# Handing out the 16 memory-projection tiles in the loop over the delta-rule chunks

## The chip, the cores and the metric

The kernel runs on one core of a Trainium2 chip. The metric is device time in microseconds of one execution. Each core has five engines with in-order instruction queues of their own: TensorE (PE, matrix products; PEld is its weight load), VectorE (DVE), ScalarE (ACT), GpSimd (POOL) and SyncE (SP), which here issues every DMA. Matrix products accumulate in PSUM banks; everything else lies in SBUF or in DRAM.

## The reference

One decoder layer over 1024 tokens of width 1024, float32. A mixer with two halves side by side (a gated delta rule over four heads, and an S5 state-space model over 512 channels with a gate), then cross-attention to 256 memory tokens, then a SwiGLU block:

```python
h = x
h = h + _mixer(_rmsnorm(h, norm_mix_g), ...)          # [delta-rule heads | S5 channels] @ w_out
h = h + _cross_attn(_rmsnorm(h, norm_x_g), mem, ...)
h = h + _swiglu(_rmsnorm(h, norm_ffn_g), ...)
return _rmsnorm(h, norm_final_g)

def _cross_attn(hn, mem, norm_mem_g, w_xq, w_xk, w_xv, w_xo):
    mn = _rmsnorm(mem, norm_mem_g)                    # 256 x 1024
    q = hn @ w_xq
    k = mn @ w_xk                                     # the memory projections:
    v = mn @ w_xv                                     # 256 x 1024 each
    s = q k^T / 16;  p = softmax(s);  return (p v) @ w_xo
```

The memory projections `k` and `v` depend on the memory tokens and on their two weights alone, not on `x`.

## The kernel before

**Numbers.** A float32 operand is split into a rounded high part and the remainder (`split`: ScalarE writes the high part, VectorE or GpSimd subtracts), and a product is three matmuls, high x high, high x low, low x high (`mm3`). `weight` loads one 128-column slice of a weight (512 KB) into `wraw` (two buffers) and splits it into `whi` and `wlo` (three buffers each); its last argument names the engine that subtracts. All these lie in the pool `wp`, which lives for the whole kernel, as do three PSUM banks `mm` in the pool `pm`.

**Order.** Instructions are written in program order, and the framework's planner (the tile context is opened with its timeline simulation) then orders each engine's queue at build time: an instruction that is earlier in the program has the higher rank, but one of lower rank goes ahead where the planner's simulated times and the free buffers allow it. On the chip each queue is worked off in that fixed order. A buffer is handed on when its readers are done, and a pool's room when the pool is closed.

**Stages around the change**, in program order in `emit`:

1. The delta-rule heads: projections (`in_tile`), `dn_a`, `dn_v`, `dn_b` for four heads; `mem_prep` before them normalises the memory tokens and leaves their split parts `mh`, `ml` in eight temporary tiles of 128 x 512 (`fsg`, `sq`, `res`, `acc0`, `acc1`), two of the eight 128-row slices in each.
2. The loop over the eight chunks of 128 tokens (line 1473). `dn_seq(c)` loads the chunk's matrices (`d_X4`, `d_kT`, `d_N3`) and goes through four dependent products with the state (lines 747, 755, 761 and 771/772), with VectorE (749, 764) and ScalarE (756) between them; `dn_tail(c - 1)` normalises and gates the chunk before and writes its split parts into `AH` and `AL`.
3. The eight S5 blocks: `s5_in` (loads `s_W`, `s_U`, `s_M`, `s_T`, matmuls, evacuation) and `s5_out` (mostly VectorE and GpSimd, lines 389 to 406; matmuls 411 and 412), with `glu_in` after every second one. The planner mixes stages 2 and 3.
4. `seq.close()` ends the chunks' pools `dp` and `sq` (`dq` in the code); the pool `kv` then opens on the same side. `glu` computes the S5 gate.
5. `mem_proj` twice, for `w_xk` and `w_xv`: eight tiles each. A tile loads and splits a weight slice (GpSimd subtracts), does 24 matmuls of 128 x 256 into an `mm` bank, is copied by ScalarE into `kst` (four buffers, in `kv`), and is stored into `memD` in DRAM.
6. `mem_load` brings the keys back from `memD` and splits them; `out_acts` forms sums and differences of the mixer's output (lines 935 to 949, in `fsg`, `res` and `sq`); `fold_k` multiplies the keys with `w_xq`; `out_pair` follows.

Of the kernel before, what the change touches and what calls it, by code (L numbers as in the profile page):

```python
# [9 lines left out]
F32 = mybir.dt.float32  # L10
F32R = mybir.dt.float32r
I32 = mybir.dt.int32
AF = mybir.ActivationFunctionType
# [5 lines left out]
P = 128  # L19
NT = 1024  # L20
HT = 512
KD = 8
NMEM = 256
# [22 lines left out]
class Kernel:  # L46
# [778 lines left out]
            ml += [two(l)[:, j] for j in range(2)]  # L825
        return mh, ml

    def mem_proj(self, kv, mem, w, dst):

        mh, ml = mem  # L830
        for m in range(KD):
            wh, wl = self.weight(self.I[w][m], KD, P, self.g)
            ps = self.pm.tile([P, HT], F32, name="mm")
            for k in range(KD):
                self.mm3(ps[:, 0:NMEM], wh[:, k], wl[:, k], mh[k], ml[k], k == 0, k == KD - 1)
            t = kv.tile([P, HT], F32, name="kst", bufs=4)[:, 0:NMEM]
            self.a.activation(out=t, in_=ps[:, 0:NMEM], func=AF.Copy)
            self.load(dst[:, m], t)

    def mem_load(self, kv, src):  # L840
        o = [kv.tile([P, KD, NMEM], F32R, name=n) for n in ("kvh", "kvl")]
# [554 lines left out]
    def emit(self, ctx):  # L1396
        tc, nc, I = self.tc, self.nc, self.I
        pool = lambda name, side="left", **k: tc.tile_pool(name=name, side=side, **k)
# [30 lines left out]
        with pool("cv", bufs=1) as cv:  # L1429
# [19 lines left out]
            mem = self.mem_prep(cv)  # L1449
            dp = seq.enter_context(pool("dp", "right", bufs=1))  # L1450
            with psum("pda", 1) as self.pda, psum("pdb", 2) as self.pb:
                with pool("dx", "right", bufs=1) as dx:
                    for hd in range(4):
                        k, q = self.in_tile(4 + hd, cv), self.in_tile(hd, cv)
# [8 lines left out]
        dq = seq.enter_context(pool("sq", "right", bufs=1))  # L1463
# [6 lines left out]
        self.turn = {}  # L1470
        with psum("ps6", 1) as self.p6, psum("pds", 1) as self.ps, psum("pdo", 2) as self.po:
            po = {}
            for c in range(9):
                if c < 8:
                    po[c] = self.dn_seq(c, dq)
                if c > 0:
                    self.dn_tail(c - 1, po[c - 1], dq, xs)
            with pool("s5b", bufs=1) as sb:
                s = self.s5_in(0, sb)
                for b in range(8):  # L1480
                    s2 = self.s5_in(b + 1, sb) if b < 7 else None
                    self.s5_out(b, sb, *s)
                    if b % 2:
                        self.glu_in(b // 2, xs)
                    s = s2
            seq.close()
            kvs = ExitStack()
            kv = kvs.enter_context(pool("kv", "right", bufs=1))
            with pool("q8", bufs=1) as q8:
                self.glu(q8, xs)  # L1490
            self.mem_proj(kv, mem, "w_xk", self.memD[0])
            self.mem_proj(kv, mem, "w_xv", self.memD[1])
        s5p.close()

        self.pa = ctx.enter_context(psum("pa", 5))
# [84 lines left out]
        for i, o in enumerate((slice(0, HT), slice(HT, HT + 256), slice(HT + 256, NT))):  # L1580
            w = o.stop - o.start
# [84 lines left out]
```

## Time and profile before

| | |
|---|---|
| median of 3 runs | 1664.36 us (1663.36 to 1666.16) |
| profiled execution | 1661.97 us, span of its instructions 1660.2 us |
| mean granted TensorE clock | 0.945 |
| busy: TensorE, VectorE, ScalarE, GpSimd | 89%, 74%, 39%, 42% of the span |
| DMA | 237.50 MB, mean 143 GB/s |

The span runs from the first to the last instruction. A busy time counts an engine's instructions that do work; waits are told as the idle time in front of an instruction, with what ended it. Stretches of the span are named in us from its start. In a table of stretches each engine has its busy us and, in brackets, its instructions; then come the granted clock of TensorE (1 is full), the mean busy share of the 16 DMA engines, and what they moved. L835 is line 835 of the kernel.

### The profile page before, as it was taken

Reading aid. Unit: us, or ns where it says so; the run is one execution under the profiler, and the core shown is the slowest. Engines: PE = TensorE matmul, PEld = TensorE weight load, DVE = VectorE, ACT = ScalarE, POOL = GpSimd, SP = SyncE. Lnnn points to the kernel's source line nnn. Section 1 sums busy time; section 2 is a strip of 40 time slices with the busy share of each in tenths; the row PEclk is TensorE's granted clock in tenths of the full one; section 3 lists DMA queues with packets and bytes.
Section 4 is the critical chain, followed back from the end, with each engine's and each line's share of the span. In section 5 each row is a group of like instructions: output and inputs, shape, how many; then the busy total and the mean of one; then the engine's idle time right before and its main releaser. Section 6 shows DMA issues by size and latency. Waiting matters only on the chain. (4 is left out here: it accounts for less than half of the span.)

```text
span 1660.2 us, 20913 instructions
## 1 busy us (share of the span) xinstructions
PE 1480.0 (89%) x7302; PEld 1230.2 (74%) x7302; DVE 1228.8 (74%) x2156; ACT 642.6 (39%) x1144; POOL 696.2 (42%) x507
## 2 busy tenths in 40 slices
PE   6887977987878958999999969999999998999985
PEld 4776766876777857878888758888888886787764
DVE  8958887976898178776555898666666658799985
ACT  5222443342445444355443433233333334533322
POOL 6084433224334554730010464333333337676554
PEclk8998989988889989999999979999999999999997
DMA  6356534345973346335524223444433446544402
GB/s 216 88 159 196 164 103 103 102 116 153 329 248 121 122 145 215 112 105 173 170 89 165 83 89 108 130 137 140 139 128 127 133 148 217 206 140 149 140 10 102
DMA packets 146617, 237.50 MB, mean 143 GB/s; under 512 B 12464, under 2 KB 79440, under 8 KB 143952
## 3 DMA queue, kind: packets, MB, share of 16 engines
q1 hardware_dynamic: 146512, 236.17, 44.4%
q8 instruction: 57, 0.93, 0.2%
q14 instruction: 48, 0.39, 0.1%
HBM read 169.69 MB, written 68.53 MB: 143 GB/s over the span
## 5 line engine op out<-in xcount | busy, mean ns | idle before, releaser
L62 ACT ACTIVATE whi<-wraw 128x1024 fp32r<-128x1024 f32 (+2 forms) x156 | 142.1, 914 | 215.7 <-PE aux L81 59.2
L79 PE MATMUL mm<-AH,whi 128*128 128x512 f32 x436 | 175.7, 403 | 2.2 <-DVE hT L1313 2.2
L81 PE MATMUL mm<-AH,wlo 128*128 128x512 f32 x420 | 168.6, 402 | 0.0
L80 PE MATMUL mm<-AL,whi 128*128 128x512 f32 x396 | 158.9, 402 | 0.0
L147 POOL TENSOR_TENSOR acc<-acc,sq 128x512 f32<-128x512 f32 (+1 forms) x41 | 53.6, 1309 | 216.6 <-ACT sq L146 215.5
L1174 POOL TENSOR_TENSOR sg<-sg,ca 128x512 f32<-128x512 f32 x44 | 64.1, 1459 | 141.2 <-DVE sg L1167 94.8
L63 DVE TENSOR_TENSOR wlo<-wraw,whi 128x1024 fp32r<-128x1024 f32 (+1 forms) x76 | 99.8, 1317 | 31.1 <-ACT whi L62 31.1
L63 POOL TENSOR_TENSOR wlo<-wraw,whi 128x1024 fp32r<-128x1024 f32 x28 | 68.3, 2440 | 130.2 <-ACT whi L62 122.2
L79 PEld LDWEIGHTS mm<-AH,whi 128*128 128x128 f32 x436 | 83.7, 192 | 22.0 <-DVE hT L1313 3.9
L80 PE MATMUL aux<-AL,whi 128*128 128x512 f32 x228 | 90.7, 398 | 5.7 <-POOL AL L63 3.4
L81 PEld LDWEIGHTS mm<-AH,wlo 128*128 128x128 f32 x420 | 80.6, 192 | 18.2 <-issue 0.4
L80 PEld LDWEIGHTS mm<-AL,whi 128*128 128x128 f32 x396 | 76.4, 193 | 16.5
L487 DVE SCALAR_TENSOR_TENSOR it<-pre,convw,it 128x512 f32<-128x512 f32 x72 | 74.8, 1039 | 6.6 <-ACT it L485 5.7
L79 PE MATMUL aux<-AH,whi 128*128 128x512 f32 x188 | 74.6, 398 | 0.3 <-ACT AH L62 0.3
L81 PE MATMUL aux<-AH,wlo 128*128 128x512 f32 x172 | 69.4, 404 | 0.0
L62 ACT ACTIVATE wlo<-graw 128x512 fp32r<-128x512 f32 x66 | 41.3, 626 | 69.8 <-PE aux L81 54.0
L81 PE MATMUL aux<-AH,whi 128*128 128x512 f32 x148 | 58.6, 396 | 0.0
L63 POOL TENSOR_TENSOR wlo<-wb,whi 128x768 fp32r<-128x768 f32 x19 | 39.6, 2084 | 44.2 <-ACT whi L62 44.2
L1172 ACT ACTIVATE ca<-ca 128x512 f32<-128x512 f32 x44 | 27.8, 632 | 77.4 <-DVE ca L1167 76.8
L79 PE MATMUL aux<-AH,wlo 128*128 128x512 f32 x132 | 53.9, 408 | 3.2 <-DVE sq L1167 3.2
L80 PEld LDWEIGHTS aux<-AL,whi 128*128 128x128 f32 x228 | 43.1, 189 | 16.8 <-POOL AL L63 4.3
L80 PE MATMUL aux<-AL,wlo 128*128 128x512 f32 x132 | 53.7, 407 | 0.0
(702 smaller groups left out, 4721.2 us busy)
## 6 DMA issues: line engine op xcount, KB each, us to landing
graw<-in_w_up SPq DMA_DIRECT2D x22, 512.0 KB
actD<-sg SPq DMA_DIRECT2D x44, 256.0 KB
acc<-in_w_down SPq DMA_DIRECT2D x42, 256.0 KB
WD<-acc SPq DMA_DIRECT2D x40, 256.0 KB
wraw<-in_w_in SPq DMA_DIRECT2D x16, 512.0 KB
d_X<-XD SPq DMA_DIRECT2D x8, 1024.0 KB
wraw<-AD SPq DMA_DIRECT2D x16, 512.0 KB
wraw<-VD SPq DMA_DIRECT2D x16, 512.0 KB
```

Of the source, the lines that this page charges most:

```text
L62: self.a.activation(out=hi, in_=src, func=AF.Copy)
L63: return (eng or self.v).tensor_tensor(out=lo, in0=src, in1=hi.bitcast(F32), op=ALU.subtract)
L79: mm(ps, wh, xh, start=first, stop=False)
L80: mm(ps, wh, xl, start=False, stop=False)
L81: mm(ps, wl, xh, start=False, stop=last)
L147: eng.tensor_tensor(out=acc, in0=acc, in1=tmp, op=ALU.add)
L487: v.scalar_tensor_tensor(out=acc, in0=pre[:, 1 + i:1 + i + HT], scalar=cw(i), in1=acc, op0=ALU.mult, op1=ALU.add)
L1172: A.activation(out=r, in_=r, func=AF.Silu)
L1174: g.tensor_tensor(out=r, in0=r, in1=sg[o], op=ALU.mult)
```

## The change

`mem_proj` becomes a generator that does one tile at each step, first the eight of `w_xk`, then the eight of `w_xv`. It is started ahead of the chunk loop and advanced by two tiles in each pass of that loop, after `dn_seq` and `dn_tail`; eight passes use up the 16 tiles. The two calls behind `glu` go. The result tile is now `mst`, 128 x 256, one buffer, in the chunks' pool `sq`, in place of `kst` with four buffers in `kv`.

```diff
-    def mem_proj(self, kv, mem, w, dst):
+    def mem_proj(self, mem, pool):
 
         mh, ml = mem
-        for m in range(KD):
-            wh, wl = self.weight(self.I[w][m], KD, P, self.g)
-            ps = self.pm.tile([P, HT], F32, name="mm")
-            for k in range(KD):
-                self.mm3(ps[:, 0:NMEM], wh[:, k], wl[:, k], mh[k], ml[k], k == 0, k == KD - 1)
-            t = kv.tile([P, HT], F32, name="kst", bufs=4)[:, 0:NMEM]
-            self.a.activation(out=t, in_=ps[:, 0:NMEM], func=AF.Copy)
-            self.load(dst[:, m], t)
+        for w, dst in (("w_xk", self.memD[0]), ("w_xv", self.memD[1])):
+            for m in range(KD):
+                wh, wl = self.weight(self.I[w][m], KD, P, self.g)
+                ps = self.pm.tile([P, HT], F32, name="mm")
+                for k in range(KD):
+                    self.mm3(ps[:, 0:NMEM], wh[:, k], wl[:, k], mh[k], ml[k], k == 0, k == KD - 1)
+                t = pool.tile([P, NMEM], F32, name="mst")
+                self.a.activation(out=t, in_=ps[:, 0:NMEM], func=AF.Copy)
+                self.load(dst[:, m], t)
+                yield
...
             po = {}
+            side = self.mem_proj(mem, dq)
             for c in range(9):
                 if c < 8:
                     po[c] = self.dn_seq(c, dq)
                 if c > 0:
                     self.dn_tail(c - 1, po[c - 1], dq, xs)
+                for _ in range(2):
+                    next(side, None)
...
             with pool("q8", bufs=1) as q8:
                 self.glu(q8, xs)
-            self.mem_proj(kv, mem, "w_xk", self.memD[0])
-            self.mem_proj(kv, mem, "w_xv", self.memD[1])
```

## The prediction

> **What bounds the kernel now.** I read the page's first part, then a table of stretches around the place of the change, then who waited for whom in the stretch that the change empties, then the order of instructions there.
>
> ```profile
> span 1660.2 us, 20913 instructions
> PE 1480.0 (89%) x7302; PEld 1230.2 (74%) x7302; DVE 1228.8 (74%) x2156; ACT 642.6 (39%) x1144; POOL 696.2 (42%) x507
> ```
>
> TensorE is busy for 89% of the span, but that is a mean over stages. The stretches show which engine is full where:
>
> ```profile
> core 0: us, PE busy (x) PEld busy (x) DVE busy (x) ACT busy (x) POOL busy (x), PEclk, DMA share, GB/s
> 403.00:420.00 17.00, 5.78 (x26) 5.12 (x24) 14.84 (x44) 2.57 (x5) 4.04 (x3) 0.62 0.88 296
> 420.00:500.00 80.00, 65.47 (x467) 61.50 (x468) 74.59 (x201) 36.62 (x94) 29.08 (x41) 0.87 0.81 280
> 500.00:520.00 20.00, 12.59 (x69) 10.77 (x68) 14.20 (x34) 10.48 (x29) 7.66 (x5) 0.83 0.68 224
> 520.00:549.30 29.30, 27.91 (x159) 23.98 (x157) 24.40 (x57) 16.91 (x40) 15.37 (x13) 1.00 0.04 15
> 549.30:591.20 41.90, 36.04 (x296) 35.21 (x297) 1.09 (x2) 15.96 (x26) 24.49 (x12) 1.00 0.50 158
> 591.20:650.00 58.80, 38.84 (x244) 34.16 (x244) 58.66 (x56) 30.42 (x50) 34.17 (x20) 0.88 0.60 193
> ```
>
> From 403 to 520 run the delta-rule chunks and the S5 blocks: VectorE is the fullest engine (74.59 of 80 us in the middle row), TensorE has gaps and a granted clock of 0.62 to 0.87. From 520 to 549 the S5 gate (`glu`) fills TensorE, 27.91 of 29.3 us. From 549.3 to 591.2 the memory projections run alone: VectorE does 1.09 us of work in 41.9. From 591 to 650 (`out_acts`, `fold_k`) VectorE is full without a gap, 58.66 of 58.8.
>
> ```profile
> engine line waited for: us in total, times, longest us
> DVE fsg L935 <- PE mm L81: 40.0, 1, 40.0
> ACT whi L62 <- DMA wraw<-in_w_xv: 18.8, 8, 4.0
> ```
>
> ```profile
> 550.57 0.69 DVE L63 TENSOR_TENSOR AL<-yy,AH 128x512 fp32r<-128x512 f32 x1 [0.87 <-ACT AH L62]
> 591.24 1.77 DVE L935 TENSOR_TENSOR fsg<-AH 128x512 f32<-128x512 f32 x1 [39.98 <-PE mm L81]
> ```
>
> This is the central reading. The split memory tokens sit in the temporary tiles `fsg`, `sq`, `res`, `acc0`, `acc1`, and `out_acts` writes its first difference (L935) into `fsg`. So VectorE, which bounds the next 59 us, sits idle for 40.0 us until the last memory matmul has read them. Its inputs were ready at about 551.
>
> **What the change removes.** Emitted among the chunks, the projections can be done before `glu` ends, and L935 then starts when L63 at 550.57 has ended: minus 40.0 us, provided that the 16 tiles are indeed done by then. What they consist of, and what is done early already:
>
> ```profile
> L54 SPq DMA_DIRECT2D wraw<-in_w_xk x8: 332/346/506, 306.3 to 414.2; - x8
> L54 SPq DMA_DIRECT2D wraw<-in_w_xv x8: 332/333/424, 555.8 to 582.9; - x8
> L54 SPq DMA_DIRECT2D memD<-kst x16: 319/320/444, 549.3 to 596.6; - x16
> L63 POOL TENSOR_TENSOR wlo<-wraw,whi 128x1024 fp32r<-128x1024 f32 x10 | 23.9, 2393 | 16.6 <-ACT whi L62 16.6
> L62 ACT ACTIVATE whi<-wraw 128x1024 fp32r<-128x1024 f32 x12 | 12.7, 1060 | 26.7 <-DMA wraw<-in_w_xv 18.8 <-DMA wraw<-in_w_xqT 4.7 <-PE mm L80 3.2
> L837 ACT ACTIVATE kst<-mm 128x256 f32<-128x256 f32 x15 | 5.5, 373 | 1.9 <-issue 1.7 <-PE mm L81 0.2
> 548.81 0.94 ACT L837 ACTIVATE kst<-mm 128x256 f32<-128x256 f32 x3
> 400.13 0.28 PE L79 MATMUL mm<-fsg,whi 128*128 128x256 f32 x1
> 402.86 0.28 PE L81 MATMUL mm<-res,wlo 128*128 128x256 f32 x1
> ```
>
> The framework's planner does not keep to program order: all eight `w_xk` loads are issued by 414, and memory matmuls run at 400. Three tiles are multiplied by 403 and wait in the three `mm` banks, three more weights are split, two more lie raw; then all stops until 548.8, where three copies come at once. What stopped them is `kst`: its pool `kv` opens only when the chunks' pools close. The new `mst` lies in the chunks' own pool, so this obstacle goes. What moves into the stretch 403 to 549 is then 13 tiles of matmuls, 10 weight splits, 16 copies, 16 stores and 8 loads.
>
> **What the moved work costs there.**
>
> *TensorE.* The two rows at 400.13 and 402.86 are the first and the last of 24 matmuls, which is one tile's count: 2.85 us a tile, 37 us for 13. The first four stretches give TensorE 111.75 us busy of 146.3, so 34.6 us idle. Demand and room nearly match: at least 2.4 us must come on top. Gaps filled whole: +0; nothing filled: +37. I take +3, because VectorE, not TensorE, sets the pace until 520, and the tiles already split can use the emptiest stretch (5.78 busy of 17 from 403). By the Trainium skill (TensorE: Matmul & The Clock Gate, "What's actually happening") the clock is halved after an idle window of about 3.4 us and freed by sustained work. The trace agrees in kind, 0.62 in the emptiest of these rows and 1.00 in the fullest; by that rule filled gaps would also speed up the old matmuls there, and this term would be 0.
>
> *GpSimd against VectorE.* `mem_proj` gives the subtraction of each split to GpSimd, 2393 ns each. Beside a long GpSimd operation VectorE stands still:
>
> ```profile
> 381.69 2.36 POOL L573 TENSOR_TENSOR d_tmp<-d_L,cst 128x1024 f32<-128x1024 f32 x1
> 384.01 2.82 POOL L63 TENSOR_TENSOR wlo<-wraw,whi 128x1024 fp32r<-128x1024 f32 x1
> 381.83 5.55 DVE L487 SCALAR_TENSOR_TENSOR it<-pre,convw,it 128x512 f32<-128x512 f32 x2 [0.79 <-ACT it L485]
> 389.13 0.74 DVE L487 SCALAR_TENSOR_TENSOR it<-pre,convw,it 128x512 f32<-128x512 f32 x1
> ...
> 407.65 2.34 POOL L63 TENSOR_TENSOR wlo<-wraw,whi 128x1024 fp32r<-128x1024 f32 x1 [4.82 <-ACT whi L62]
> 407.42 0.22 DVE L670 TENSOR_TENSOR d_R<-d_R,d_X 128x56 f32<-128x56 f32 x1
> 408.93 1.15 DVE L670 TENSOR_TENSOR d_R<-d_R,d_X 128x64 f32<-128x64 f32 x1
> ```
>
> Two VectorE operations that take 0.74 us alone took 5.55 beside two GpSimd ones: 4.07 us lost, 2.0 for each. At 408.93 the loss beside one split was 0.93 (1.15 against 0.22). Now these splits cost nothing, since VectorE is idle at 549 to 591 anyway; moved, they fall where it is 93% full. Bounds for 10 splits: 0 (all in VectorE's gaps) and 24 (each holds it for its whole 2.4 us). I take 1.6 each, between the two rows and nearer to the 2.0, because S5's stream of two-input operations leaves a split few moments without one: +16. By the Trainium skill (SBUF — State Buffer, "Who interferes with whom") a VectorE instruction with two SBUF inputs and a GpSimd one that reads SBUF exclude each other for a whole instruction, and whichever issues first wins. The trace agrees: at 408.93 the operation waits out the split. By that rule the term would be up to +24 where GpSimd is always first and +0 where VectorE always is, and the sum -13 to -37.
>
> *DMA and SyncE.* Eight loads of 512 KB and sixteen stores of 128 KB are 6.3 MB. At the rate of the 403 to 420 row (296 GB/s at a share of 0.88, so 336 at full) that is 19 us of DMA time, and the four rows leave 52 us of it idle, most of that after 520. Until 500 the loads of the chunks and of S5 share at 0.81 to 0.88, so their latency grows; bounds 0 and 19, I take +2. SyncE's 24 issues at 0.33 us are 8 us of a queue with gaps, but a store waits there for its copy, and the loads of `d_X4`, `d_kT`, `d_N3`, `s_M`, `s_T` queue behind it: same term.
>
> *ScalarE.* Ten `whi` at 1.06 us and 16 copies at 0.37 are about 17 us on an engine busy for 66.6 of 146.3: +0, hidden in its 80 idle us; what if it has to wait is the third rival.
>
> *What starts earlier.* With `wp` free, the first `w_xqT` weights can be loaded and split while `glu` runs. VectorE does these splits at the head of its full stretch. Bounds 0 and 5; I take -2.
>
> After 650 nothing is touched; the rest moves earlier as a block.
>
> **Sum:** -40 + 3 + 16 + 2 + 0 - 2 = -21 us. The profiled execution took 1661.97 us (span 1660.2 and 1.8 around it), so 1641.0 on its own scale. The median of the runs, 1664.36, is 2.4 above it: 1643.4, given as 1643. Against no change 0.2% (3.3 us) can be told.
>
> **The rivals.**
>
> *Hidden whole.* The splits fall beside VectorE work that doesn't collide, or VectorE is first and GpSimd waits (the split at 384.01 took 2.82 against 2.39, so that happens). Then -40 - 2 with at most +8: 1622 to 1630, say 1624. For it: splits already at 400 ran free; against it: VectorE's 93%.
>
> *Tiles come late.* The planner works with times of its own, and lets the low-ranked end of the 16 tiles slip into 520 to 549, where TensorE has 1.4 us left. Six such tiles cost 6 x 2.85 = 17 us there without the gaps' help, on top of the 16 for the splits and the 2 for DMA, and the -2 is lost: -40 + 35 = -5: 1659. A step further, the tiles stay behind `glu` as they are now, the change does nothing it says: 1664. For it: the planner already decides the order now; against: it did hurry these very tiles ahead at 400, as far as buffers went.
>
> *One buffer for the results: slower.* `kst` has four buffers, `mst` one. Each copy must wait until the store before it has landed, and ScalarE takes its work in order; behind a waiting copy stands the evacuation on which each chunk's state hangs (L756, eight of them 13 us apart).
>
> ```profile
> L756 ACT ACTIVATE d_R<-ds x8: 590/604/636, 440.0 to 532.7; 128x512 f32<-128x512 f32 x8
> 601.74 0.32 SPq L54 DMA_DIRECT2D kst<-memD  x1
> 605.61 0.63 ACT L62 ACTIVATE kvh<-kst 128x512 fp32r<-128x512 f32 x1 [2.12 <-DMA kst<-memD]
> ```
>
> The nearest row to such a store's landing is the load at 601.74, waited for until 605.61: 3.9 us. If copies come in pairs, as the loop hands them out, 15 waits of up to 3.9 are 58 us, and 21 are enough to eat the sum: it decides from 1.4 us lost per copy. At 2.5 us each: +37, 1680. Against it: two tiles of 2.85 us per chunk of 13 leave time for a store to land.
>
> **How the numbers follow.** Forecast, gain less the collision: 0.50, own range 1632 to 1654. Hidden whole: 0.25. Late tiles with a small gain: 0.10. No effect: 0.05. One buffer: 0.10. The range leaves out the slower case and the lowest corner: 1620 to 1660. Faster by over 0.2%: 0.50 + 0.25 + 0.10 = 0.85; within: 0.05; slower: 0.10.
>
> **What would show it.** Right: the 40.0 us wait of `fsg` L935 for a matmul is gone or below 5; memory matmuls and `memD` stores lie between 410 and 530; VectorE operations of S5 stand beside `wlo` splits with 1 to 2 us more than their kind; the S5 blocks and `glu` end some 15 to 20 us later than now. Hidden: `glu` ends within 8 us of 549. Late tiles: `memD` stores after 530. One buffer: ScalarE's waits name the store of `mst`. The prediction is wrong if VectorE loses less than 0.8 or more than 2.4 us per split, or if the chunks themselves are drawn out by TensorE standing in memory tiles when a chunk's matmul is ready.

## The result and the profile after

| | median | runs | profiled execution, span |
|---|---|---|---|
| before | 1665.26 us | 1663.36 to 1667.36 (4) | 1661.97, 1660.2 us |
| changed | 1648.39 us | 1641.72 to 1651.58 (4) | 1650.67, 1649.0 us |

The ratio is 0.9893, 95% interval 0.9857 to 0.9929: 16.9 us faster by the medians, 11.3 by the two profiled executions, which all balances below go by. The head of the page of the changed kernel:

```profile
span 1649.0 us, 20913 instructions
PE 1483.9 (90%) x7302; PEld 1233.3 (75%) x7302; DVE 1249.9 (76%) x2156; ACT 643.5 (39%) x1144; POOL 693.1 (42%) x507
```

With the same 2156 instructions VectorE is busy for 21.1 us more (1228.8 before). The stretches of the changed kernel, cut at the same times as before:

```profile
core 0: us, PE busy (x) PEld busy (x) DVE busy (x) ACT busy (x) POOL busy (x), PEclk, DMA share, GB/s
403.00:420.00 17.00, 10.15 (x64) 9.69 (x63) 13.69 (x41) 3.27 (x7) 6.30 (x5) 0.70 0.92 299
420.00:500.00 80.00, 66.61 (x505) 64.14 (x504) 66.15 (x153) 35.67 (x92) 36.01 (x37) 0.87 0.78 279
500.00:520.00 20.00, 17.10 (x125) 16.91 (x126) 14.03 (x42) 9.87 (x23) 5.97 (x7) 0.83 0.73 248
520.00:549.30 29.30, 21.68 (x169) 20.67 (x168) 26.43 (x68) 12.37 (x35) 13.18 (x11) 0.94 0.51 165
549.30:591.20 41.90, 38.13 (x217) 32.37 (x216) 30.14 (x39) 25.43 (x44) 18.29 (x12) 0.96 0.45 143
591.20:650.00 58.80, 47.99 (x259) 40.63 (x258) 55.84 (x57) 29.31 (x48) 35.75 (x22) 0.88 0.49 163
```

The empty stretch of VectorE (1.09 us in 549 to 591) is gone, 30.14 now. But from 420 to 500 it got through 153 instructions, not 201, and was even less busy (66.15 against 74.59). What VectorE waited for between 403 and 655, the longest first:

```profile
engine line waited for: us in total, times, longest us
DVE AL L63 <- ACT AH L62: 10.2, 6, 3.3
DVE d_R L665 <- DMA d_R<-LD: 8.3, 1, 8.3
DVE wlo L63 <- ACT whi L62: 5.2, 2, 5.0
DVE s_Z L391 <- POOL s_m L390: 4.6, 1, 4.6
DVE d_L L764 <- PE ds L761: 3.2, 2, 2.5
DVE s_X L406 <- POOL s_m L403: 2.3, 1, 2.3
DVE AL L63 <- PE aux L81: 2.1, 1, 2.1
DVE d_N L692 <- PE db L684: 2.0, 1, 2.0
DVE s_m L389 <- DMA s_M<-SD: 1.4, 1, 1.4
DVE d_R L749 <- PE ds L747: 1.4, 1, 1.4
```

The 40.0 us wait for the memory matmuls has gone, whole. Of the waits left, those for `LD` (9.0 before) and for `AH` (6.2 before) were there already. New or longer are those for TensorE (9.4 us in all, against 0.2 before beside the 40.0), for the S5 products of GpSimd (L391 and L406: 6.9, against 1.2) and for ScalarE. The S5 scans (L395), spread from 417.0 to 490.3 before, now end at 536.9:

```profile
L395 DVE TENSOR_TENSOR_SCAN s_S<-s_m,s_Z x32: 391/398/2581, 418.5 to 536.9; 128x128 f32<-128x128 f32 x32
L54 SPq DMA_DIRECT2D memD<-mst x16: 320/354/1142, 418.5 to 575.5; - x16
L54 SPq DMA_DIRECT2D AD<-kst x16: 319/320/424, 585.3 to 622.1; - x16
```

So much of the gain was given back: S5 ends 47 us later and the gate follows it (the last start of its L904, now L906, goes from 548.4 to 597.5), but `fold_k` (stores to `AD`) starts at 585.3, 28 us earlier than the 613.7 before, and overlaps with the gate. One balance holds all this. I take the stretch from 403 to the last of the `out_pair` matmuls with a `T` operand in the bank `mm` (line 80): 450 VectorE instructions in both kernels. Before, then changed:

```profile
403.00:718.10 315.10, 254.73 (x1541) 225.99 (x1540) 238.02 (x450) 142.34 (x290) 159.95 (x120) 0.91 0.54 183
```

```profile
403.00:708.50 305.50, 258.27 (x1566) 230.05 (x1565) 256.44 (x450) 143.44 (x290) 162.69 (x122) 0.90 0.56 190
```

VectorE: 18.4 us more busy, 28.0 us less idle (77.1 to 49.1), sum -9.6 us, and -11.2 at the end of the span. Two questions follow: are the 18.4 us really GpSimd's doing, and why did the idle time fall by 28 and not by 40?

The waits in this stretch answer the second in part. Beside the 40.0 us, VectorE's waits for TensorE grew by 9.2 us, for GpSimd by 3.2 (7.3 to 10.5) and for ScalarE by 2.4 (15.1 to 17.5), and those for DMA, `LD` aside, fell by 2.6: together 12. One wait for TensorE shows what the moved matmuls do. ScalarE has finished L756 at 504.07, but TensorE stands in a memory tile from 503.03 to 507.9 and starts the chunk's product L761 only at 507.96, while VectorE idles:

```profile
503.47 0.60 ACT L756 ACTIVATE d_R<-ds 128x512 f32<-128x512 f32 x1 [3.34 <-PE ds L755]
509.06 1.12 DVE L764 SCALAR_TENSOR_TENSOR d_L<-d_L,dn_al,ds 128x128 f32<-128x128 f32 x4 [2.55 <-PE ds L761]
```

From 504.0 to 507.2 TensorE is busy without a gap at a granted clock of 0.50.

Three rows of the changed kernel show the loss beside GpSimd; two scans take 2.89 us beside a split, and four take 1.36 without one:

```profile
420.82 2.42 POOL L63 TENSOR_TENSOR wlo<-wraw,whi 128x1024 fp32r<-128x1024 f32 x1 [4.70 <-ACT whi L62]
420.94 2.89 DVE L395 TENSOR_TENSOR_SCAN s_S<-s_m,s_Z 128x128 f32<-128x128 f32 x2
432.77 1.36 DVE L395 TENSOR_TENSOR_SCAN s_S<-s_m,s_Z 128x128 f32<-128x128 f32 x4
```

And a group shows a wait for GpSimd. It stands 6.05 us with a memory split at the head of its queue, waiting for ScalarE's `whi`; behind it stand S5's products L390, whose inputs are there (VectorE's twin L389 ran at 441.48); VectorE, which needs them in L391, idles for 4.57 us. Of L390's delay after 441.48, 2.25 us are the split's wait and 2.3 its own work:

```profile
441.48 0.76 DVE L389 TENSOR_TENSOR s_m<-s_M,s_P 128x256 f32<-128x256 f32 x2 [1.41 <-DMA s_M<-SD]
442.60 1.05 ACT L62 ACTIVATE whi<-wraw 128x1024 fp32r<-128x1024 f32 x1
443.73 2.35 POOL L63 TENSOR_TENSOR wlo<-wraw,whi 128x1024 fp32r<-128x1024 f32 x1 [6.05 <-ACT whi L62]
446.05 1.40 POOL L390 TENSOR_TENSOR s_m<-s_M,s_P 128x256 f32<-128x256 f32 x2
446.80 0.93 DVE L391 TENSOR_TENSOR s_Z<-s_m,s_m 128x256 f32<-128x256 f32 x1 [4.57 <-POOL s_m L390]
```

### The profile page after: what moved, and what is told of

Same layout as the page of the kernel before. It is cut to its first block, busy times and chain, and to the rows that moved or that the text cites. A ratio compares the mean times of both kernels' runs of the same rounds, so it can differ in the third digit from the quotient of the medians.

```text
span 1649.0 us, 20913 instructions
## 1 busy us (share of the span) xinstructions
PE 1483.9 (90%) x7302; PEld 1233.3 (75%) x7302; DVE 1249.9 (76%) x2156; ACT 643.5 (39%) x1144; POOL 693.1 (42%) x507
## 5 line engine op out<-in xcount | busy, mean ns | idle before, releaser
L80 PEld LDWEIGHTS aux<-AL,whi 128*128 128x128 f32 x228 | 43.0, 189 | 17.5 <-POOL AL L63 4.6
```

Source lines behind the costliest of these rows:

```text
L80: mm(ps, wh, xl, start=False, stop=False)
```

## The experiments

Theories: A, VectorE loses its time beside GpSimd's splits and behind them (later parted into L, the time beside them, and Q, their waiting at the head of GpSimd's queue); B, TensorE's moved matmuls draw the stage out; C, the tiles' rank ahead of S5 delays S5. All of them at a glance (the busy time of VectorE and the start of the last S5 scan are those of the profiled execution):

| kernel | median us | ratio to before, 95% interval | VectorE busy us | last S5 scan |
|---|---|---|---|---|
| before | 1660.9 to 1665.3 | 1 | 1228.8 | 490.3 |
| changed | 1648.39 | 0.9893 (0.9857 to 0.9929) | 1249.9 | 536.9 |
| lo_on_vector | 1625.47 | 0.9775 (0.9756 to 0.9794) | 1248.2 | 503.0 |
| lo_by_scalar | 1632.58 | 0.9813 (0.9789 to 0.9837) | 1229.6 | 506.5 |
| one_product | 1641.18 | 0.9877 (0.9853 to 0.9901) | 1249.1 | 529.5 |
| after_s5 | 1647.59 | 0.9912 (0.9891 to 0.9932) | 1254.6 | 522.0 |
| two_buffers | 1653.17 | 0.9949 (0.9929 to 0.9968) | 1242.2 | 537.9 |
| before_gpsimd | 1673.86 | 1.0082 (1.0064 to 1.0100) | 1249.1 | 509.5 |
| before_vector | 1656.51 | 0.9979 (0.9965 to 0.9994) | 1240.3 | 499.0 |
| vector_plus_gpsimd | 1646.09 | 0.9907 (0.9888 to 0.9926) | 1266.5 | 518.3 |
| vector_tiny_gpsimd | 1641.67 | 0.9867 (0.9848 to 0.9886) | 1249.4 | 528.4 |
| vector_tiny_free | 1624.99 | 0.9769 (0.9753 to 0.9784) | 1240.7 | 507.1 |
| vector_after_s5 | 1639.44 | 0.9840 (0.9826 to 0.9854) | 1244.6 | 517.6 |
| every_other | 1657.24 | 0.9971 (0.9957 to 0.9985) | 1245.1 | 544.2 |

**Who subtracts.**

```diff
-                wh, wl = self.weight(self.I[w][m], KD, P, self.g)
+                wh, wl = self.weight(self.I[w][m], KD, P)
```

> The changed kernel, but the remainder of each memory weight is subtracted by VectorE instead of GpSimd. Theory A (the loss in the chunk stage is VectorE standing beside GpSimd's splits, and S5's GpSimd work queued behind them): ten splits of 2.4 us on GpSimd cost VectorE about 18 us more busy time; on VectorE they cost 10 x 1.2 = 12 us, and the queue on GpSimd is clear: 5 to 10 us faster than the changed kernel's 1648, 1638 to 1643. Theory B (TensorE's 37 us of moved matmuls draw the stage out; GpSimd is harmless): VectorE only gets 12 us of extra work in its full stage: 1655 to 1660. Theory C (the tiles' rank ahead of S5 in the plan delays S5, whoever splits): no change, 1644 to 1652.

1625.47 us: the best but for one that differs by nothing that can be told, and 23 us below the changed kernel's median, 20 by the two ratios, where 5 to 10 were expected. It speaks for A against B and C, but lies outside A's range too. VectorE's busy time in the span is as in the changed kernel (16 subtractions of its own in place of the time lost beside GpSimd's). The page and the stretch:

```profile
span 1621.2 us, 20906 instructions
403.00:680.40 277.40, 245.41 (x1569) 220.21 (x1568) 247.25 (x453) 142.49 (x290) 140.23 (x110) 0.95 0.61 206
```

Idle are 277.4 - 247.25 = 30.2 us, against 49.1, and busy 247.25 against 256.44: of 28.1 us, 18.9 are idle time and 9.2 busy time. (The cut at 403 flatters this kernel a little: the wait for `LD` ends at 401.3 here and at 405.4 in the changed kernel. Counted from there, the idle times are 30.4 and 46.7.) The waits for TensorE are 1.4 us here, with the same matmuls moved, and the granted clock in the stage is 0.95 against 0.90; whether the clock is a cause of the shorter stage or follows from it isn't shown.

**The subtraction left out.**

```diff
-                wh, wl = self.weight(self.I[w][m], KD, P, self.g)
+                raw, wh, wl = ...                       # the tiles that weight() makes
+                self.load(raw, self.I[w][m])
+                self.a.activation(out=wh, in_=raw, func=AF.Copy)
+                self.a.activation(out=wl, in_=raw, func=AF.Copy)
```

> The changed kernel, but the low part of each memory weight is written by ScalarE as a second copy of the weight, so the subtraction is left out and neither GpSimd nor VectorE takes part. Theory A: the 18 us of VectorE and the queueing on GpSimd go, ScalarE has 17 us more and room for it: 1622 to 1632. Theory B: no change, 1644 to 1652. Theory C: no change, 1644 to 1652.

1632.58 us, just above A's range. VectorE's busy time falls by 20.3 us to 1229.6, almost the 1228.8 of before: nearly the whole excess was time beside the splits. All 16 are gone here; from 403 on, where 12 of them ran in the changed kernel, the busy time falls by 18.1 us (930.1 to 912.0), 1.5 for each.

```profile
403.00:684.00 281.00, 247.69 (x1563) 221.36 (x1562) 234.34 (x439) 152.09 (x301) 136.69 (x110) 0.94 0.59 203
```

The idle time in the stage is 281.0 - 234.34 = 46.7 us, as much as in the changed kernel, though no memory split stands in GpSimd's queue. ScalarE, with 16 more copies, is now what VectorE waits for (13.4 us for `AH` against 5.5 in lo_on_vector).

**TensorE's part.**

```diff
-                    self.mm3(ps[:, 0:NMEM], wh[:, k], wl[:, k], mh[k], ml[k], k == 0, k == KD - 1)
+                    self.te.matmul(ps[:, 0:NMEM], wh[:, k], mh[k], start=k == 0, stop=k == KD - 1)
```

> The changed kernel, but each memory tile does only high x high, 8 matmuls instead of 24: the two products with a low part are left out, all splits, loads, copies and stores stay. 16 x 16 x 0.119 = 30 us less on TensorE. Theory A: TensorE's share is small, 0 to 6 us faster: 1642 to 1648. Theory B: 20 to 30 us faster: 1618 to 1628. Theory C: 5 to 10 faster, because S5 waits less behind the tiles: 1638 to 1643.

1641.18 us, 7 us below the changed kernel by the medians and 3 by the ratios, whose intervals overlap. B's 20 to 30 us don't show. But the experiment took less off TensorE than it meant to: its busy time falls by 17.2 us and not by 30 (1483.9 to 1466.7), while its granted clock in the stage falls from 0.90 to 0.85. So B falls in its size, and a smaller part of TensorE stays possible.

**The rank.** All tiles behind the S5 blocks, ahead of `seq.close()`:

```diff
-                for _ in range(2):
-                    next(side, None)
...
+            for _ in side:
+                pass
             seq.close()
```

> The changed kernel, but the generator is not advanced in the chunk loop: all 16 tiles are emitted behind the S5 blocks, still ahead of the closing of the chunks' pools and of the S5 gate, with the same result buffer. The tiles then rank behind S5 in the plan and may still fill gaps from 403 on. Theory C: S5 keeps its pace, the tiles use what is left: faster than the changed kernel, 1632 to 1642. Theory A: the splits stand beside VectorE's work in the same stage as now: about the same, 1643 to 1653. Theory B: TensorE is as full: the same, 1644 to 1652.

1647.59 us: as the changed kernel, with stores to `memD` from 422.5 to 567.8. C falls as put; handing the tiles out in the chunk loop is not what made them early. A result buffer in a pool that is open is enough.

**The single buffer.**

```diff
-                t = pool.tile([P, NMEM], F32, name="mst")
+                t = pool.tile([P, NMEM], F32, name="mst", bufs=2)
```

> The changed kernel with two result buffers mst instead of one. The rival of the single buffer: ScalarE's waits for the store before hold up the chunks' evacuations, so a second buffer gives 8 us or more: below 1640. Theories L and Q (GpSimd's splits cost the time, by standing beside VectorE, or by waiting at the head of GpSimd's queue): ScalarE's waits for a store are 4.1 us in all in the changed kernel, so 0 to 4 us faster: 1643 to 1650.

1653.17 us, not faster but, if anything, slower. This rival falls. VectorE's busy time is 7.7 us below the changed kernel's, with the same splits on GpSimd; so the loss beside them depends on the order too.

**GpSimd's work alone, in the old order.**

```diff
                     self.dn_tail(c - 1, po[c - 1], dq, xs)
+                if 1 <= c <= 5:
+                    for _ in range(4):
+                        scr = dq.tile([P, 4, P], F32, name="scr")
+                        src = [self.cst[:, o:o + P].unsqueeze(1).to_broadcast([P, 4, P]) for o in (C_ID, C_BD)]
+                        self.g.tensor_tensor(out=scr, in0=src[0], in1=src[1], op=ALU.mult)
```

> The kernel before, with the projections where they were, and 20 extra GpSimd products of 128x512 (about 1.2 to 1.4 us each, about as much GpSimd time as ten memory splits; two constant SBUF inputs, nothing to wait for, result unused) handed out four with each of the chunks 1 to 5. Theory L (two-input GpSimd work beside VectorE's full stage costs VectorE its duration): VectorE's busy time +15 to +24, time +10 to +20: 1672 to 1684. Theory Q (a split costs by waiting for ScalarE with S5's work behind it in GpSimd's queue): these wait for nothing, GpSimd has room: 1660 to 1667.

1673.86 us, +13 on its own base of 1660.88. L holds: operations that need nothing and give nothing come with 13 us more.

```profile
PE 1489.4 (89%) x7302; PEld 1237.7 (74%) x7302; DVE 1249.1 (75%) x2156; ACT 642.6 (38%) x1144; POOL 722.7 (43%) x527
L1482 POOL TENSOR_TENSOR scr<-cst x20: 1260/1334/1516, 413.3 to 464.5; 128x512 f32<-128x512 f32 x20
```

GpSimd has 26.5 us more, VectorE 20.3: each 1.33 us operation takes about 1.0 from VectorE.

**VectorE's splits without the move.** The kernel before, with the edit of lo_on_vector.

> The kernel before, with VectorE instead of GpSimd subtracting in the 16 memory splits. If what VectorE's splits gained in the changed kernel is about the moved place (theories L and Q): ten of them run where VectorE is idle anyway, and TensorE waited there 6.7 us for GpSimd's splits: 0 to 7 us faster than before, 1656 to 1664. If it is independent of the place (the six early splits among the heads, or faster splits as such): as much as there, 20 us faster, 1640 to 1646.

1656.51 us, 4 us faster. So most of lo_on_vector's 20 us belong to the moved place.

**GpSimd's work put back.** On lo_on_vector, in the chunk loop:

```diff
+                if 1 <= c <= 5:
+                    for _ in range(8):
+                        scr = dq.tile([P, 2, P], F32, name="scr")
+                        ...                             # two constant inputs, 128x256
+                        self.g.tensor_tensor(out=scr, in0=src[0], in1=src[1], op=ALU.mult)
```

> The changed kernel with VectorE subtracting in the memory splits, and 40 extra GpSimd products of 128x256 (about 0.73 us each, 29 us in all; constant SBUF inputs, nothing to wait for, result unused) handed out eight with each of the chunks 1 to 5. Theory L: VectorE's busy time +15 to +20 and the time with it, 1637 to 1645. Theory Q: nothing waits at the head of GpSimd's queue, each extra operation holds S5's work for 0.7 us at most: 1624 to 1630.

1646.09 us, 20.6 above lo_on_vector and 1 above L's range, VectorE's busy time 18.3 above. L again. Its idle time stays low, though, 295.9 - 269.28 = 26.6 us:

```profile
403.00:698.90 295.90, 255.21 (x1569) 227.92 (x1570) 269.28 (x460) 141.11 (x290) 173.44 (x150) 0.91 0.57 194
```

So with GpSimd as full as by the splits, but without their waits, the idle time of the changed kernel (49.1) doesn't come back. That left Q as a candidate; these operations are also shorter (0.79 us in the median against 2.4).

**A wait without the work.** On lo_on_vector, beside each memory split:

```diff
+                scr = pool.tile([P, 16], F32, name="scr")
+                self.g.tensor_tensor(out=scr, in0=raw[:, 0, 0:16], in1=wh[:, 0, 0:16].bitcast(F32), op=ALU.subtract)
```

> The changed kernel with VectorE subtracting in the memory splits, and with each of them an extra GpSimd subtraction of only 128x16 of the same weight and its high part (result unused): it waits for ScalarE at the head of GpSimd's queue just as a split did, but holds GpSimd for some 0.1 us instead of 2.4. Theory L alone (only the time that GpSimd works beside VectorE costs): 0 to 3 us slower than without it, 1624 to 1630. Theory Q as the second half (VectorE's extra idle time of about 19 us comes from splits waiting at the head of GpSimd's queue, with S5's products behind them): VectorE's idle time in the stage +10 to +19 and the time with it, 1635 to 1645.

1641.67 us: sixteen operations of 0.2 to 1.2 us, 16 us slower than lo_on_vector. VectorE's idle time in the stage is 290.7 - 249.8 = 40.9 us, 10.7 more, within Q's forecast. What GpSimd waited for in this kernel, where the operations ran, and what VectorE waited for longest:

```profile
POOL scr L837 <- ACT whi L62: 19.3, 6, 6.9
L837 POOL TENSOR_TENSOR scr<-wraw,whi x16: 221/412/1208, 410.3 to 494.5; 128x16 f32<-128x16 f32 x16
DVE wlo L63 <- ACT whi L62: 11.7, 5, 3.8
```

**The same without the wait**, on constants (`in0=self.cst[:, 0:16], in1=self.cst[:, C_BD:C_BD + 16]`):

> As the kernel with the 128x16 GpSimd subtractions, but these read constants and wait for nothing. If the waiting at the head of GpSimd's queue made the difference (theory Q): as fast as with VectorE's splits alone, a ratio to before of 0.976 to 0.981, 1622 to 1631. If any 16 extra instructions on GpSimd change the planned order enough (theory P, the plan itself is worth some 15 us either way): a ratio of 0.984 or more, 1638 and up.

1624.99 us. The same 16 instructions cost nothing that can be told where they wait for nothing. They run from 418.2 to 427.1, and VectorE's wait for `whi` is short:

```profile
DVE wlo L63 <- ACT whi L62: 2.2, 3, 1.4
```

The size agrees with Q: 16 operations with almost no work in them are 16 us slower where they wait for ScalarE (ratios 0.9867 and 0.9769). The traces don't bear Q out as the path. First, the pair differs in more than the wait: without the dependency all 16 ran within 9 us early in the stage, and about a tenth of VectorE's 2172 instructions stand in another place of its order. Second, VectorE hardly waited for GpSimd's S5 products in either (L391 and L406: 0.7 us with the wait, 2.6 without). What grew is its wait for ScalarE's `whi` at its own splits, 2.2 to 11.7 us. So the 16 us can be the order's, whole or in part; that the waiting GpSimd delayed ScalarE's inputs in turn is not excluded.

**Two that don't fit.** Both edits at once, VectorE's splits and the late rank:

> Both edits: VectorE subtracts in the memory splits, and all 16 tiles are emitted behind the S5 blocks instead of in the chunk loop. With GpSimd out of it, the tiles' rank could matter again. Theory C (rank ahead of S5 costs S5 its pace): 5 to 15 us faster than with VectorE's splits in the chunk loop, 1610 to 1620. Theories L and Q (what costs is GpSimd, not the rank): within 6 us of it, 1619 to 1631.

1639.44 us, 14 slower than lo_on_vector by the medians and 11 by the ratios, outside both expectations: with GpSimd out of it the rank does matter, and to be behind S5 is worse. VectorE waits 13.7 us for ScalarE's `whi` there, against 2.8, as in the tiny kernel with the wait. The last, the two engines by turns:

```diff
-                wh, wl = self.weight(self.I[w][m], KD, P, self.g)
+                wh, wl = self.weight(self.I[w][m], KD, P, self.g if m % 2 else None)
```

> The changed kernel with VectorE subtracting in the even tiles and GpSimd in the odd ones. Theory L with Q: halfway between 0.9893 (GpSimd in all) and 0.9775 (VectorE in all): a ratio of 0.981 to 0.986, 1632 to 1641. Theory P (plan alone): anywhere between 0.97 and 0.99, with VectorE's idle time and not its busy time off the halfway point.

1657.24 us, far from halfway. VectorE's busy time in the stage is 247.6 us, its idle time 305.5 - 247.6 = 57.9, the most of all kernels with the move:

```profile
403.00:708.50 305.50, 254.06 (x1564) 225.87 (x1563) 247.60 (x441) 142.60 (x290) 150.64 (x116) 0.91 0.54 187
POOL wlo L63 <- ACT whi L62: 17.0, 5, 6.7
```

Its splits on GpSimd wait 17.0 us for `whi`, against 23.0 in the changed kernel, but VectorE waits for S5's products only 0.6 us; its longest waits are for ScalarE's `AH` (13.8) and for TensorE's L761 (6.9). That doesn't fit Q.

Every edit here makes the planner draw up a new order. Over the kernels with the move, VectorE's idle time in the stage is 39 to 56 us with all 16 splits on GpSimd (one_product, after_s5, changed, two_buffers) and 27 to 47 with none (vector_plus_gpsimd, lo_on_vector, the two tiny kernels, vector_after_s5, lo_by_scalar): the two groups overlap. I take this scatter, some 15 us either way, for the order's doing; that is argued, not shown. So L stands on VectorE's busy time in three kernels (18 to 20 us each, where edits that leave L as it is moved it by up to 8). Q, the waiting in GpSimd's queue, is seen in single places such as the group at 441.48, and its share of the rest is not shown.

## Why the prediction was right

Forecast 1643 in 1620 to 1660, measured 1648.39; forecast -21 us, measured -16.9. The two large terms were right in mechanism. The nearness of the sum is in part luck: on the profiled executions, which show the terms, 1641.0 was forecast and 1650.67 measured, so the terms together were some 10 us short, 2 to 5 of them in the second term and the rest in the small ones.

- *The wait of 40.0 us.* Right: L937, the old L935, starts at 570.4 without a wait worth listing.
- *GpSimd against VectorE, +16.* Right in mechanism and nearly in size: +18.4 in the stage, +21.1 in the span. Taking the splits off both engines brought 20.3 back. Per split the forecast was 1.6 us; the excess over the ten moved ones is 1.8 to 2.1, the removal gives 1.5. The range's upper end, 24, held.
- *TensorE, +3.* Too small in this trace: VectorE's waits for TensorE grew by 9.2 us in the stage, and at 504 to 509 the chunk stood behind a memory tile, which the prediction named as a sign of being wrong. The chunks themselves are drawn out by 8 us (the L756 rows span 92.7 us before and 101.1 now), and TensorE's L755 waits 19.1 us for VectorE's L749, against 0.8, so VectorE has a share in that too. In lo_on_vector the same matmuls cost VectorE 1.4 us of waiting; how much of the 9.2 is the order's isn't shown. That filled gaps would speed TensorE up didn't show: the granted clock in the stage was 0.91 before and 0.90 after.
- *DMA and SyncE, +2, ScalarE, +0, and what starts earlier, -2.* No run isolates these. VectorE's waits for ScalarE grew by 2.4 us in the stage. A term was missing: the prediction counted a split's 2.4 us and not what is queued behind it while it waits for `whi`; VectorE's waits for GpSimd grew by 3.2 us. The earlier `fold_k` gave some back.
- *Places.* S5 and `glu` were to end 15 to 20 us later: it was 47 and 49. Stores were to lie between 410 and 530: they lie from 418.5 to 575.5, and eight of the 16 copies come after 531. That was the mark of the rival with late tiles, and it was partly true, without its price. A likely reason is that `fold_k` now overlaps with the gate, so that what TensorE lost there it gained behind; no run tests this.
- *One buffer.* ScalarE waited 4.1 us for stores in all, and a second buffer bought nothing.

By the Trainium skill (SBUF — State Buffer, "Who interferes with whom") a VectorE instruction with two SBUF inputs contends with a GpSimd one that reads SBUF. The runs agree, for work put in and work taken out: 26.5 us more of GpSimd work with two SBUF inputs took 20.3 us from VectorE, and without the 16 splits 20.3 came back.

## What to carry to other kernels

Moving work into a stage's gaps is priced by what it does to that stage's fullest engine, the shared operand path and the queues included, not by the gap's size. When an in-order engine is given an operation that waits for another, count everything that stands behind it, and where a planner redraws the order, expect a scatter of its own (here about as large as the effects sought). And ask again, after the move, which engine should do the moved work: GpSimd's subtraction cost 4 us where VectorE was idle and 20 where it was full, and changing it took the gain from 17 to 37 us.

## What the runs showed of the hardware

A GpSimd product with two constant SBUF inputs of 128x512 took 1.33 us, and VectorE's busy time grew by about 1.0 us for each (20.3 for 20, in before_gpsimd), though nothing depends on them. The loss shows as busy time of VectorE, not as a wait. A memory tile squeezed into a gap of TensorE ran at a granted clock of 0.50 (504.0 to 507.2 in the changed kernel), so it took longer there than the 2.85 us for which the prediction counted it: 23 of its 24 matmuls took 4.9 us.
